# More landing buffers for stored sums, a merge by token halves and halved low parts in an encoder layer's kernel

## The chip, the cores and the metric

The kernel runs on one core of a Trainium2 chip. The metric is the device time of one launch in microseconds. The engines are named as in the profile: PE multiplies matrices, DVE, ACT and POOL work on vectors, SP issues every DMA of this kernel. Each engine takes its instructions in a fixed order.

## The reference

One encoder layer is computed for a prompt of 512 tokens and for a sample of 1024 tokens with the same weights, all in float32. Two attention branches, each 512 wide, are gated, projected to 1024 channels, merged and projected once more. Cut to what matters here:

```python
h = rmsnorm(x, norm_g)
qa, ka, va, za, qb, kb, vb, zb, ga, gb = jnp.split(h @ w_in, np.cumsum(SPLITS)[:-1], axis=-1)
...
oa = neighbourhood_attention(qa, ka, va, rpb_a) * jax.nn.silu(za)
oa = oa @ w_o_a
...
ob = window_gqa_attention(qb, kb, vb, t5_table, sink_b) * jax.nn.silu(zb)
ob = ob @ w_o_b
merged = jax.nn.sigmoid(ga) * oa + jax.nn.sigmoid(gb) * ob
return x + merged @ w_out
```

Queries and keys are normalised per head before the scores. The neighbourhood attention adds a learned bias per offset of rows and columns, the windowed attention a bias per distance and a sink.

## The kernel before

**Products.** A float32 matrix product is made of three matmuls in the faster format fp32r. Each operand is split into a high part (ACT copies it, L602, L1170) and a low part (DVE or POOL subtracts the high part from the original, L607, L1175). The three matmuls are high by high, high by low, low by high; in the dense stages these are L1288, L1289 and L1290 of `product`, and one such step covers 128 of the contracted channels and 512 tokens. Weights land in `raw` (4 buffers) or, for attention, in `w` (128x768) and are split into `whi` and `wlo` (6 buffers each).

**Stages.** In order of time: attention of the prompt (to about 216 us), its dense stages (to 399), attention of the sample (399 to 787), and the sample's dense stages: the z gates (787 to 830), the merge gates g (830 to 966), the merge (966 to 1054) and the output projection (1054 to 1132). Work of two stages overlaps where data allow; some products of g and z for the sample (the "fill") are made in gaps of its attention.

**Pairs.** z, g and the output are made in pairs of output blocks by `pair_strassen`: seven products p1 to p7 replace eight, and for that both weights and tokens are needed as block sums too. The weight sums are s1 to s4 (L1164, tile S). The token sums of the sample are four blocks T of four 128-channel parts each. They were written to DRAM as t_d early on, and `stored_sums` (L1231) loads each part from t_d into a landing buffer `U` of four (L1240) and splits it into the high and low tiles of T. The T tiles have eight buffers, which u and the sums of the merged result (m_d) use later. For the first z pair p1 is already there (`kept`), so the pair begins with p2, which reads h itself, then three products that read T, and so on; p7 reads h itself again.

**u and merge.** The gated attention result u goes to DRAM (u_d) in `store` (L1512) and comes back in 16 loads, 8 chunks by two halves of the tokens (n), through `ot` (first half) and `fr` (second half), chunk by chunk with both halves in turn (L1672 to L1679). The merge loop (L1700) takes an output block m at a time in the order 0, 4, 1, 5 and so on; for each it splits two weight tiles, makes the products of both halves for both branches, loads g back (L1721), multiplies, adds and splits. After every second block `merged_sums` makes the sums m_d of the pair.

**Order.** The class `Flow` takes the whole program as operations with a priority, a choice of engines with an estimated duration for each, and the values they make, read or hold. `run` plays them through on a model of the engines and so fixes engine and order of every instruction ahead of time. Tiles of tags such as U, T, raw, whi, wlo and w are handed out in turn, as their buffers come free. A change in one duration or priority can therefore move instructions anywhere behind it, also in code that the change does not touch.

Of the kernel before, what the change touches and what calls it, by code (L numbers as in the profile page):

```python
# [10 lines left out]
F32 = mybir.dt.float32  # L11
# [29 lines left out]
P = 128  # L41
# [313 lines left out]
def encoder_kernel(  # L355
# [238 lines left out]
    def att_weights(src, n, prio, engs=("pool", "dve"), place=None, after=()):  # L594

        st, at, new = place or (f.value(wpool, [P, 768], F32, "w32", W32), 0, True)
        hi = f.value(wpool, [P, 768], F32R, "whi", 6)
        lo = f.value(wpool, [P, 768], F32R, "wlo", 6)
        sv = lambda: st.t[:, at : at + n]
        ld = f.dma(lambda: nc.sync.dma_start(sv(), src), 512 * n, prio, after=after, **({"new": [st]} if new else {"hold": [st]}))  # L600
        a = f.op(
            (("act", ACT_(n) + 40),), lambda e: act.activation(hi.t[:, :n], sv(), AF.Copy),  # L602
            prio, new=[hi], hold=[st], after=[ld],
        )

        def emit(e):
            engines[e].tensor_tensor(lo.t[:, :n], sv(), hi.t[:, :n].bitcast(F32), op=ALU.subtract)  # L607

        f.op(
            tuple((e, {"pool": POOL_, "dve": DVE_}[e](n)) for e in engs), emit, prio, new=[lo], use=[hi], hold=[st], after=[a],  # L610
        )
        return hi, lo
# [523 lines left out]
    def dense_phase(geo, hh, hl, h_ops, o_stores, exps_done, start, opened, tp, up, p0, p1, p2, x_t, y_t, classic, fill, after_gates=None, side=None):  # L1136
# [93 lines left out]

        def stored_sums(prio, d, after):  # L1231

            tv, ops = {}, {}
            for j in (1, 2, 0, 3):
                tv[j] = tuple(f.value(tp, [P, 4, nh], F32R, "T", 8) for _ in range(2))
                vh, vl = tv[j]
                for k in range(4):
                    st = tile_("U", 4)
                    dma(
                        lambda st=st, j=j, k=k: nc.sync.dma_start(st.t, d[j, k]), 512 * nh, prio, new=[st],  # L1240
                        after=after(j, k),
                    )
                    ops[j, k] = split(
                        lambda vh=vh, k=k: vh.t[:, k], lambda vl=vl, k=k: vl.t[:, k], lambda st=st: st.t, nh, prio,
                        (vh, k == 0), (vl, k == 0), [st],
                    )
# [77 lines left out]
        def pair_strassen(srcs, post, prio, mov_h, mov_t, seed=None, last=False, kept=None):  # L1324
# [40 lines left out]
            else:  # L1365
# [4 lines left out]
                result(0, 0, p1, mul(1, mov_h(1, 0)))  # L1370
            add(u2, p1, mul(2, mov_t(1)))
# [5 lines left out]
            if not last:  # L1377
                result(0, 1, u4, mul(6, mov_h(1, 1)))
# [18 lines left out]

        def spare(tag):
            return f.value(wpool, [P, nh], F32, tag, {"fc": 1}.get(tag, 2))
# [271 lines left out]
        if not short:  # L1671
            for c in range(8):  # L1672
                for n in halves:
                    st = f.value(wpool, [P, nh], F32, "fr", 2) if n else tile_("ot", n_ot)
                    dma(
                        lambda st=st, c=c, n=n: nc.sync.dma_start(st.t, u_d[c, :, half[n]]), 512 * nh, 10 + c // 4,
                        new=[st], after=stores["u", c, n],
                    )
                    split_u(c, n * nh, nh, st, 10 + c // 4)  # L1679
# [20 lines left out]
        for q in range(8):  # L1700
            m = q if short else q // 2 + 4 * (q % 2)
            prio = 12 + q
            ws = []
            for br in range(2):
                raw = load_raw(w_g[m, 4 + br], prio - 2)
                ws.append(weight_tiles([raw], 4, prio - 0.5)[0])
            for n in halves:
                gs_ = []
                for br in range(2):
# [6 lines left out]
                    m_done[q, n] = product(ps, ws[br], movs, prio, True, True)  # L1716
                    tag, bufs = (("C", n_c), ("ot", n_ot) if short else ("U", 4))[br]
                    g = tile_(tag, bufs) if short or br or m < 4 else spare("fl" if n else "fh")
                    turn = [] if short or br or m < 4 else [m_done[max(q - 2, 0), 0]]
# [18 lines left out]
            if not short and m >= 4:  # L1738
# [203 lines left out]
```

## Time and profile before

| | |
|---|---|
| time before, median of 3 runs | 1135.88 us (1134.05 to 1137.46) |
| time of the profiled execution | 1136.88 us |
| its span | 1135.1 us |
| granted TensorE clock, mean | 1.00 |
| ACT busy, share of span | 653.7 us, 58% |
| POOL busy, share of span | 327.1 us, 29% |
| bytes moved by DMA | 186.11 MB, mean 164 GB/s |

The span is the time from the first to the last instruction in the profile; the launch has 1.8 us around it. A row of a timeline gives start, duration, engine, line, operation and, in brackets, how long the engine had been idle and what it then waited for. Matmuls are pipelined: their durations overlap, and what counts is the distance of their starts. In rows of waits the numbers are the total, how often, and the longest. In the rows of one line's operations the three durations are the least, the median and the greatest in ns.

### The profile page before, as it was taken

What the parts mean: (1) busy time and instruction counts of PE and PEld (TensorE: products, weight loads), DVE (VectorE), ACT (ScalarE), POOL (GpSimd) and SP (SyncE); (2) the same over time, 40 slices, a digit from 0 to 9 for tenths busy, and PEclk for the clock granted to TensorE, in tenths of its full rate; (3) what the DMA queues carried; (4) which work ended last, traced back from release to release, by engine and by line L of the source; (5) the groups of instructions that cost most, each with busy time, mean ns of one, the idle gap of its engine ahead of it and who ended that gap; (6) DMA issues with size and microseconds to landing.
All of it is one profiled execution on the core that took longest, in us unless ns stands there. A gap on an engine that the chain in (4) does not pass through costs nothing.

```text
span 1135.1 us, 18686 instructions
## 1 busy us (share of the span) xinstructions
PE 1121.6 (99%) x6079; PEld 973.9 (86%) x6079; DVE 863.8 (76%) x1995; ACT 653.7 (58%) x1498; POOL 327.1 (29%) x432
## 2 busy tenths in 40 slices
PE   8999999999999999999999999999999999999998
PEld 6999988888888889999899988988788888788887
DVE  5888797587765468887868888885888866779874
ACT  6777987644433246574759888876534434522440
POOL 4654433000010044433414344420033221124221
PEclk9999999999999999999999999999999999999999
DMA  7854533488786422121312314244958645868982
GB/s 261 273 157 139 183 115 103 110 262 260 241 276 196 159 91 72 29 79 29 91 32 84 82 38 112 57 131 127 300 187 244 218 167 180 297 219 281 302 279 93
DMA packets 139108, 186.11 MB, mean 164 GB/s; under 512 B 29897, under 2 KB 68561, under 8 KB 139010
## 3 DMA queue, kind: packets, MB, share of 16 engines
q1 hardware_dynamic: 139010, 184.91, 51.4%
q8 instruction: 48, 0.79, 0.3%
q14 instruction: 50, 0.41, 0.1%
HBM read 138.71 MB, written 50.88 MB: 167 GB/s over the span
## 4 chain that ended last, share of the span: by engine, by line
PE 89%; DMA 4%; DVE 4%; ACT 1%; issue 1%; SPq 0%; POOL 0%; DVEq 0%; POOLq 0%; ACTq 0%
PE p L761 25%; PE x L1288 8%; PE x L1290 8%; PE x L1289 8%; PE x L1063 5%; PE x L1026 5%; PE x L934 5%; PE d L1288 4%; PE d L1289 4%; PE d L1290 4%; PE p L1289 4%; PE p L1290 4%; PE p L1288 4%; PE x L861 2%; DMA ot<-u_d 1%
## 5 line engine op out<-in xcount | busy, mean ns | idle before, releaser
L761 PE MATMUL p<-whi,hh 128*128 128x384 f32 x384 | 133.6, 348 | 0.0
L761 PE MATMUL p<-whi,hl 128*128 128x384 f32 x384 | 132.4, 345 | 0.0
L761 PE MATMUL p<-wlo,hh 128*128 128x384 f32 x384 | 132.2, 344 | 0.0
L978 ACT ACTIVATE sb<-sb,mx 128x384 f32<-128x384 f32 (+1 forms) x192 | 107.7, 565 | 22.9 <-DVE mx L969 22.6
L1170 ACT ACTIVATE whi<-raw 128x512 fp32r<-128x512 f32 (+1 forms) x136 | 79.4, 599 | 67.4 <-PE x L1289 46.3
L1289 PE MATMUL x<-T,whi 128*128 128x512 f32 x284 | 110.7, 390 | 0.3 <-DVE T L1175 0.2
L1288 PE MATMUL x<-T,whi 128*128 128x512 f32 x284 | 110.6, 390 | 0.0
L1290 PE MATMUL x<-T,wlo 128*128 128x512 f32 x284 | 110.5, 389 | 0.0
L761 PE MATMUL p<-whi,hb 128*128 128x384 f32 x384 | 107.8, 346 | 0.0
L1037 DVE TENSOR_TENSOR pp<-x,pp 128x512 fp32r<-128x512 f32 (+1 forms) x136 | 82.6, 639 | 20.3 <-ACT pp L1032 19.2
L1175 DVE TENSOR_TENSOR wlo<-raw,whi 128x512 fp32r<-128x512 f32 (+1 forms) x109 | 73.3, 682 | 26.5 <-ACT whi L1170 26.0
L1175 POOL TENSOR_TENSOR wlo<-raw,whi 128x512 fp32r<-128x512 f32 (+1 forms) x27 | 32.1, 1199 | 172.9 <-ACT whi L1170 160.2
L799 POOL TENSOR_TENSOR rs_r<-rs_v,mhalf 128x4 f32<-128x4 f32 (+1 forms) x72 | 79.9, 1109 | 5.7
L1032 ACT ACTIVATE pp<-x 128x512 fp32r<-128x512 f32 (+1 forms) x136 | 70.9, 561 | 18.2 <-PE x L1026 17.1
L792 POOL TENSOR_SCALAR rs_v<-ss 128x4 f32<-128x4 f32 (+1 forms) x72 | 26.0, 361 | 185.1 <-DVE ss L785 181.7
L1063 PE MATMUL x<-pp,v 128*128 128x256 f32 (+1 forms) x368 | 76.6, 322 | 0.0
L1288 PE MATMUL x<-hh,whi 128*128 128x512 f32 x196 | 76.4, 390 | 0.1
L1290 PE MATMUL x<-hh,wlo 128*128 128x512 f32 x196 | 76.3, 389 | 0.0
L1289 PE MATMUL x<-hl,whi 128*128 128x512 f32 x196 | 76.2, 389 | 0.0
L761 PEld LDWEIGHTS p<-whi,hl 128*128 128x128 f32 x384 | 72.8, 190 | 1.3 <-issue 1.0
L761 PEld LDWEIGHTS p<-whi,hh 128*128 128x128 f32 x384 | 73.0, 190 | 1.1 <-issue 0.5
L761 PEld LDWEIGHTS p<-wlo,hh 128*128 128x128 f32 x384 | 72.9, 190 | 0.9 <-issue 0.5
(381 smaller groups left out, 3011.9 us busy)
## 6 DMA issues: line engine op xcount, KB each, us to landing
raw<-in_w_g_dram SPq DMA_DIRECT2D x84, 256.0 KB
w<-in_w_att_dram SPq DMA_DIRECT2D x46, 384.0 KB
raw<-in_w_z_dram SPq DMA_DIRECT2D x40, 256.0 KB
ot<-o_d SPq DMA_DIRECT2D x36, 256.0 KB
raw<-in_w_out_dram SPq DMA_DIRECT2D x36, 256.0 KB
g_d<-C SPq DMA_DIRECT2D x34, 256.0 KB
fr<-in_w_g_dram SPq DMA_DIRECT2D x28, 256.0 KB
out_dram<-C SPq DMA_DIRECT2D x19, 256.0 KB
```

Of the source, the lines that this page charges most:

```text
L761: pe.matmul(ps.t[:, :GW], part[u](k), mv.t[:, c], start=k == 0 and m == 0, stop=k == KC - 1 and m == 2,)
L799: lambda e: nc.gpsimd.tensor_tensor(r.t[:, :nn], rv.t[:, :nn], mhalf[:, :nn], op=ALU.pow),
L934: pe.matmul(pss[2 * pair + i].t[:, :width], q.t[rows, u, at : at + P], kv[:, tiles[0] : tiles[-1] + 1 : step], start=n == 0, stop=n == 2,)
L978: act.activation(sb.t[:, :width], sb.t[:, :width], AF.Exp, bias=mx.t[:, i : i + 1], scale=-1.0, accum_out=sm.t[:, i : i + 1],)
L1032: lambda e, pt=pt, pp=pp, nn=nn: act.activation(pp.t[:, 0, :nn], pt.t[:, :nn], AF.Copy),
L1037: lambda e, pt=pt, pp=pp, nn=nn: dve.tensor_tensor(pp.t[:, 1, :nn], pt.t[:, :nn], pp.t[:, 0, :nn].bitcast(F32), op=ALU.subtract),
L1063: pe.matmul(out(), v.t[:, vs], mv(), start=first, stop=last)
L1170: (("act", ACT_(n)),), lambda e: act.activation(hi(), src(), AF.Copy), prio,
L1175: lambda e: engines[e].tensor_tensor(lo(), src(), hi().bitcast(F32), op=ALU.subtract), prio,
L1288: pe.matmul(out, hi.t[:, cs], mh(), start=first and k == 0, stop=False, **more)
L1289: pe.matmul(out, hi.t[:, cs], ml(), start=False, stop=False, **more)
L1290: pe.matmul(out, lo.t[:, cs], mh(), start=False, stop=last and k == len(ws) - 1, **more)
```

## The change

The change has five parts. In the code `short` is true for the prompt and false for the sample, and `here` is true for the pairs of z whose first product was kept in a tile, `prio` being 0 for the first of them.

1. `att_weights`: the low part of an attention weight tile is made by two subtractions of half the width, each of which may go to POOL or DVE by itself.
2. `stored_sums`: for t_d, the parts k = 1 and k = 3 land in the buffers `fh` (2) and `w32` (2, the attention weights' own) in place of U, so eight landing buffers serve in place of four. The loads now also wait for the operation `opened`, which opens the stage's tiles.
3. `pair_strassen`: in the first z pair the seventh product, which reads h and the weight sum s4, is made right behind p2, ahead of the products that read T.
4. The loads of u come back by halves: the first half of all eight chunks, then the second; they land in `fr`, `fh`, `fl` and `ot` by turns, and their priorities follow.
5. The merge goes by turns (m, n): blocks k and k+4 of the first half, then both of the second half. The weights of both blocks are kept for that. The wait that holds back g's loads for m >= 4 is now for the third product from the last.

```diff
@@ -603,12 +603,15 @@
             prio, new=[hi], hold=[st], after=[ld],
         )
 
-        def emit(e):
-            engines[e].tensor_tensor(lo.t[:, :n], sv(), hi.t[:, :n].bitcast(F32), op=ALU.subtract)
-
-        f.op(
-            tuple((e, {"pool": POOL_, "dve": DVE_}[e](n)) for e in engs), emit, prio, new=[lo], use=[hi], hold=[st], after=[a],
-        )
+        for i in range(2):
+            c = slice(i * n // 2, (i + 1) * n // 2)
+            f.op(
+                tuple((e, {"pool": POOL_, "dve": DVE_}[e](n // 2)) for e in engs),
+                lambda e, c=c: engines[e].tensor_tensor(
+                    lo.t[:, c], st.t[:, at : at + n][:, c], hi.t[:, c].bitcast(F32), op=ALU.subtract
+                ),
+                prio, use=[hi], hold=[st], after=[a], **({"into": [lo]} if i else {"new": [lo]}),
+            )
         return hi, lo
 
     def expand_ops(geo, prios, after):
@@ -1228,6 +1231,9 @@
 
             return moving_sums(tv, ops)
 
+        def spare(tag):
+            return f.value(wpool, [P, nh], F32, tag, {"fc": 1}.get(tag, 2))
+
         def stored_sums(prio, d, after):
 
             tv, ops = {}, {}
@@ -1235,13 +1241,13 @@
                 tv[j] = tuple(f.value(tp, [P, 4, nh], F32R, "T", 8) for _ in range(2))
                 vh, vl = tv[j]
                 for k in range(4):
-                    st = tile_("U", 4)
+                    st = spare(("fh", "w32")[k // 2]) if not short and d is t_d and k % 2 else tile_("U", 4)
                     dma(
-                        lambda st=st, j=j, k=k: nc.sync.dma_start(st.t, d[j, k]), 512 * nh, prio, new=[st],
-                        after=after(j, k),
+                        lambda st=st, j=j, k=k: nc.sync.dma_start(st.t[:, :nh], d[j, k]), 512 * nh, prio, new=[st],
+                        after=[*after(j, k), *([opened] if d is t_d else [])],
                     )
                     ops[j, k] = split(
-                        lambda vh=vh, k=k: vh.t[:, k], lambda vl=vl, k=k: vl.t[:, k], lambda st=st: st.t, nh, prio,
+                        lambda vh=vh, k=k: vh.t[:, k], lambda vl=vl, k=k: vl.t[:, k], lambda st=st: st.t[:, :nh], nh, prio,
                         (vh, k == 0), (vl, k == 0), [st],
                     )
             return moving_sums(tv, ops)
@@ -1368,6 +1374,7 @@
                     (("act", ACT_(sn)),), lambda e: act.activation(p1.t, a.t[:, :sn], AF.Copy), prio, new=[p1], use=[a]
                 )
                 result(0, 0, p1, mul(1, mov_h(1, 0)))
+            ps7 = mul(6, mov_h(1, 1)) if here and not prio else None
             add(u2, p1, mul(2, mov_t(1)))
             add(u3, u2, mul(3, mov_t(2)))
             b = mul(4, mov_t(0))
@@ -1375,7 +1382,7 @@
             result(1, 1, u3, b)
             result(1, 0, u3, mul(5, mov_t(3)), ALU.subtract)
             if not last:
-                result(0, 1, u4, mul(6, mov_h(1, 1)))
+                result(0, 1, u4, ps7 or mul(6, mov_h(1, 1)))
                 return
 
             c = seed(0, sn, sn, u4, prio)
@@ -1394,9 +1401,6 @@
                 last_op = f.ops[-1]
                 post(0, nh + s.start, nh // 2, c, False, prio, s.start, [last_op])
 
-
-        def spare(tag):
-            return f.value(wpool, [P, nh], F32, tag, {"fc": 1}.get(tag, 2))
 
         def pairs_apart(jobs, prio, mov_h, mov_t, late, seed=None, ready=()):
 
@@ -1669,14 +1673,15 @@
         if after_gates:
             after_gates()
         if not short:
-            for c in range(8):
-                for n in halves:
-                    st = f.value(wpool, [P, nh], F32, "fr", 2) if n else tile_("ot", n_ot)
+            for n in halves:
+                for c in range(8):
+                    st = spare(("fr", "fh", "fl")[c % 4]) if c % 4 < 3 else tile_("ot", n_ot)
+                    pr = 10 + n + c // 4 / 2
                     dma(
-                        lambda st=st, c=c, n=n: nc.sync.dma_start(st.t, u_d[c, :, half[n]]), 512 * nh, 10 + c // 4,
+                        lambda st=st, c=c, n=n: nc.sync.dma_start(st.t, u_d[c, :, half[n]]), 512 * nh, pr,
                         new=[st], after=stores["u", c, n],
                     )
-                    split_u(c, n * nh, nh, st, 10 + c // 4)
+                    split_u(c, n * nh, nh, st, pr)
 
 
         m_ops, m_vals, m_stores, m_done = {}, {}, {}, {}
@@ -1697,15 +1702,18 @@
                     lambda vd=vd, j=j: nc.sync.dma_start(m_d[j, k], vd.t), 512 * sn, prio, after=[o], hold=[vd],
                 )
 
-        for q in range(8):
-            m = q if short else q // 2 + 4 * (q % 2)
-            prio = 12 + q
-            ws = []
-            for br in range(2):
-                raw = load_raw(w_g[m, 4 + br], prio - 2)
-                ws.append(weight_tiles([raw], 4, prio - 0.5)[0])
-            for n in halves:
+        turns, m_ws, m_prods = [(m, 0) for m in range(8)], {}, []
+        if not short:
+            turns = [(k + 4 * i, n) for k in range(4) for n in range(2) for i in range(2)]
+        for q, (m, n) in enumerate(turns):
+            if True:
+                prio = 12 + q * 8 / len(turns)
                 gs_ = []
+                if m not in m_ws:
+                    m_ws[m] = [
+                        weight_tiles([load_raw(w_g[m, 4 + br], prio - 2)], 4, prio - 0.5)[0] for br in range(2)
+                    ]
+                ws = m_ws[m]
                 for br in range(2):
                     ps = bank(next(tags))
                     vh, vl = uv[br, n]
@@ -1713,10 +1721,10 @@
                         (lambda k=k, vh=vh: vh.t[:, k], lambda k=k, vl=vl: vl.t[:, k], u_ops[br, n, k], [vh, vl])
                         for k in range(4)
                     ]
-                    m_done[q, n] = product(ps, ws[br], movs, prio, True, True)
+                    m_prods.append(product(ps, ws[br], movs, prio, True, True))
                     tag, bufs = (("C", n_c), ("ot", n_ot) if short else ("U", 4))[br]
                     g = tile_(tag, bufs) if short or br or m < 4 else spare("fl" if n else "fh")
-                    turn = [] if short or br or m < 4 else [m_done[max(q - 2, 0), 0]]
+                    turn = [] if short or br or m < 4 else m_prods[-3:-2]
                     dma(
                         lambda g=g, br=br, m=m, n=n: nc.sync.dma_start(g.t, g_d[br, m, :, half[n]]), 512 * nh,
                         prio - 0.5, new=[g], after=[*stores["g", br, m, n], *turn],
@@ -1735,7 +1743,7 @@
                     prio, (hh, None), (hl, None), [a], after=h_reads,
                 )
                 m_vals[m, n] = a
-            if not short and m >= 4:
+            if not short and m >= 4 and n:
                 merged_sums(m - 4, prio)
             if side:
                 side(12 + q)
```

The matmuls stay the same in number. `Flow` gives the following new orders.

The first place is SP at the end of the sample's attention, where the loads of t_d begin; o_d is the attention result, raw the next weights, u_d the gated result. Before:

```order
L1527 DMA ot<-o_d_80 128x512 x2
L1240 DMA U<-t_d 128x512 x3
L1252 DMA raw<-in_w_z_dram 128x512 x2
L1240 DMA U<-t_d 128x512
L1512 DMA u_d_93<-C 128x512
L1527 DMA ot<-o_d_80 128x8x64 x2
L1512 DMA u_d_93<-C 128x512
L1252 DMA raw<-in_w_z_dram 128x512
L1240 DMA U<-t_d 128x512
L1252 DMA raw<-in_w_z_dram 128x512
L1240 DMA U<-t_d 128x512 x3
L1527 DMA ot<-o_d_80 128x8x64 x2
```

With the change (the two w names are landing buffers of the attention weights):

```order
L1531 DMA ot<-o_d_80 128x512 x2
L1246 DMA U<-t_d 128x512
L1246 DMA fh<-t_d 128x512
L1246 DMA U<-t_d 128x512
L1246 DMA w_10532<-t_d 128x512
L1258 DMA raw<-in_w_z_dram 128x512 x2
L1516 DMA g_d_94<-fc 128x512
L1516 DMA u_d_93<-C 128x512
L1531 DMA ot<-o_d_80 128x8x64
L1258 DMA raw<-in_w_z_dram 128x512
L1246 DMA U<-t_d 128x512
L1246 DMA fh<-t_d 128x512
```

The loads of t_d stood in groups of three, one, one and three, with stores of u between them; now the first four stand together, and the second four (to `w_10589`) and the third four follow one another. On PE, 13 steps of the fill and a first product stand between the last product of attention and the first product of this stage that reads h, where there were 2, and 24 steps that read h stand ahead of the first one that reads T, where there were 16.

The second place is SP towards the end of the g gates, where loads of u begin. Before:

```order
L1676 DMA ot<-u_d_93 128x512 x2
L1252 DMA raw<-in_w_g_dram 128x512
L1676 DMA fr<-u_d_93 128x512 x2
L1676 DMA ot<-u_d_93 128x512
L1721 DMA U<-g_d_94 128x512 x2
L1676 DMA ot<-u_d_93 128x512
L1512 DMA g_d_94<-C 128x512
L1252 DMA raw<-in_w_g_dram 128x512
L1721 DMA U<-g_d_94 128x512
L1676 DMA fr<-u_d_93 128x512
L1512 DMA g_d_94<-C 128x512
L1676 DMA fr<-u_d_93 128x512
```

With the change:

```order
L1516 DMA g_d_94<-C 128x512
L1258 DMA raw<-in_w_g_dram 128x512
L1681 DMA fr<-u_d_93 128x512
L1681 DMA fh<-u_d_93 128x512
L1681 DMA fl<-u_d_93 128x512
L1681 DMA ot<-u_d_93 128x512
L1258 DMA raw<-in_w_g_dram 128x512
L1681 DMA fr<-u_d_93 128x512
L1681 DMA fl<-u_d_93 128x512
L1729 DMA U<-g_d_94 128x512
L1681 DMA ot<-u_d_93 128x512
L1729 DMA U<-g_d_94 128x512 x2
```

Ahead of the first row here stood four loads of u, the first two chunks with both halves, and the other twelve follow chunk by chunk, from the first row on. With the change all eight loads of the first half stand ahead of this place, in the two buffers each of `fr`, `fh`, `fl` and `ot`, and the rows here are those of the second half.

The third place is POOL in the middle of the sample's attention: low parts of two attention weights (the w names), the reciprocal roots rs of the head norms, and the scaling of attention weights sb. Before:

```order
L799 TENSOR_TENSOR rs_r<-rs_v,mhalf 128x4
L607 TENSOR_TENSOR wlo<-w_6990,whi 128x768
L607 TENSOR_TENSOR wlo<-w_7007,whi 128x768
L1175 TENSOR_TENSOR fl<-fr,fh 128x512
L1008 TENSOR_TENSOR sb<-sb,rs 128x384 x3
L792 TENSOR_SCALAR rs_v<-ss 128x4
L799 TENSOR_TENSOR rs_r<-rs_v,mhalf 128x4
```

With the change:

```order
L610 TENSOR_TENSOR wlo<-w_6377,whi 128x384
L1079 TENSOR_TENSOR ot__7039<-ot__7039 64x2x128
L610 TENSOR_TENSOR wlo<-w_6391,whi 128x384
L795 TENSOR_SCALAR rs_v<-ss 128x4
L802 TENSOR_TENSOR rs_r<-rs_v,mhalf 128x4
L610 TENSOR_TENSOR wlo<-w_7058,whi 128x384 x2
L610 TENSOR_TENSOR wlo<-w_7112,whi 128x384
```

Two subtractions of 768 columns in a row have become three of 384, the fourth being DVE's, with norm roots ahead of them, and single halves stand further ahead. In all, POOL had 12 such subtractions of 768 columns and has 39 of 384; DVE had 36 and has 57. The scalings sb on POOL go from 27 to 41.

## The prediction

> **What bounds the kernel now.** The page comes first: is any engine free to give?
>
> ```profile
> span 1135.1 us, 18686 instructions
> PE 1121.6 (99%) x6079; PEld 973.9 (86%) x6079; DVE 863.8 (76%) x1995; ACT 653.7 (58%) x1498; POOL 327.1 (29%) x432
> ```
>
> PE is busy in 99% of the span, and the change takes no matmul away. So it can win only what PE loses in gaps, and the page's 1135.1 - 1121.6 = 13.5 us is their sum with the start and the tail. The list of what PE waited for says which gaps these are:
>
> ```profile
> PE x L1799 <- DMA rb<-in_norm_row_dram: 4.6, 1, 4.6
> PE x L861 <- DVE qk L816: 2.6, 3, 1.1
> PE d L1289 <- DVE T L1175: 0.8, 2, 0.4
> ```
>
> The 4.6 us at the start have nothing to do with the change. The rest is small, and this list counts a gap only behind the modelled end of a matmul. Matmuls overlap, so I read losses from starts in the timeline of PE instead. The first z pair of the sample:
>
> ```profile
> 811.13 0.50 PE L1288 MATMUL x<-T,whi 128*128 128x512 f32 x1
> 811.85 0.50 PE L1289 MATMUL x<-T,whi 128*128 128x512 f32 x1 [0.22 <-DVE T L1175]
> ...
> 814.50 0.39 PE L1288 MATMUL x<-T,whi 128*128 128x512 f32 x1
> 815.00 0.50 PE L1289 MATMUL x<-T,whi 128*128 128x512 f32 x1
> 815.34 0.39 PE L1290 MATMUL x<-T,wlo 128*128 128x512 f32 x1
> ...
> 818.77 0.39 PE L1290 MATMUL x<-T,wlo 128*128 128x512 f32 x1
> 818.99 0.39 PE L1288 MATMUL d<-T,whi 128*128 128x512 f32 x1
> 819.73 0.50 PE L1289 MATMUL d<-T,whi 128*128 128x512 f32 x1 [0.35 <-DVE T L1175]
> ...
> 822.35 0.39 PE L1288 MATMUL d<-T,whi 128*128 128x512 f32 x1
> 823.17 0.50 PE L1289 MATMUL d<-T,whi 128*128 128x512 f32 x1 [0.43 <-DVE T L1175]
> ```
>
> Starts stand 0.23 apart when nothing is late (818.77 to 818.99). Four steps are late, by 0.49, 0.27, 0.51 and 0.59, and one start after each comes 0.11 late as well (815.00 to 815.34): 1.86 + 0.44 = **2.3 us**. All four are the second matmul of a step, which reads the low part of a block sum T. Its chain is a DMA from t_d into a U buffer, the high part on ACT, the low part on DVE. The timelines of SP and ACT show why it is late:
>
> ```profile
> 794.26 3.45 SPq L1512 DMA_DIRECT2D u_d<-C  x1
> ...
> 799.25 1.33 SPq L1240 DMA_DIRECT2D U<-t_d  x3
> ...
> 802.27 2.43 SPq L1512 DMA_DIRECT2D u_d<-C  x1
> ...
> 805.76 3.11 SPq L1240 DMA_DIRECT2D U<-t_d  x4
> ```
>
> ```profile
> 810.44 1.25 ACT L1170 ACTIVATE T<-U 128x512 fp32r<-128x512 f32 x2 [3.48 <-DMA U<-t_d]
> ...
> 818.12 2.55 ACT L1170 ACTIVATE T<-U 128x512 fp32r<-128x512 f32 x4 [3.59 <-DMA U<-t_d]
> ```
>
> SP issues in its fixed order. Four U buffers let only four loads be ahead; SP stands 3.11 us at the third four, since they wait for the split of the four before, and 3.45 and 2.43 us at stores of u between them. ACT then sits idle for the loads. The last of the four has a second cause:
>
> ```profile
> 820.31 2.81 DVE L1175 TENSOR_TENSOR T<-U,T 128x512 fp32r<-128x512 f32 x2
> ```
>
> ```profile
> 821.28 1.30 POOL L1175 TENSOR_TENSOR wlo<-S,whi 128x512 fp32r<-128x512 f32 x1 [0.44 <-DMA raw<-in_w_z_dram]
> ```
>
> Two DVE subtractions of 0.69 took 2.81 while one POOL subtraction ran. The same shows in attention, where it makes PE's largest gap there:
>
> ```profile
> 544.21 0.42 DVE L1080 TENSOR_TENSOR ot__6987<-ot__6987 64x256 f32<-64x256 f32 x1
> ...
> 547.39 1.86 DVE L1080 TENSOR_TENSOR ot__7030<-ot__7030 64x256 f32<-64x256 f32 x1
> ```
>
> ```profile
> 547.12 3.81 POOL L607 TENSOR_TENSOR wlo<-w,whi 128x768 fp32r<-128x768 f32 x2 [0.26 <-ACT whi L602]
> ```
>
> ```profile
> 548.21 0.33 PE L761 MATMUL p<-wlo,hh 128*128 128x384 f32 x1
> 548.39 0.34 PE L761 MATMUL p<-whi,hl 128*128 128x384 f32 x1
> 549.73 0.41 PE L861 MATMUL x<-ident,qk 128*128 128x128 f32 x2 [1.00 <-DVE qk L816]
> ```
>
> A DVE multiply of 0.42 takes 1.86, until about the end of the first of POOL's two 768-wide subtractions; the qk multiply stands behind it on DVE, and PE, in 0.18 steps before, loses 1.34 - 0.18 = **1.2 us**. Third, the merge stage:
>
> ```profile
> 966.89 0.63 ACT L1170 ACTIVATE T<-ot 128x512 fp32r<-128x512 f32 x1 [1.45 <-DMA ot<-u_d]
> ```
>
> ```profile
> 969.73 0.39 PE L1290 MATMUL p<-T,wlo 128*128 128x512 f32 x1
> 970.37 0.49 PE L1288 MATMUL p<-T,whi 128*128 128x512 f32 x1 [0.25 <-ACT T L1170]
> 971.10 0.50 PE L1289 MATMUL p<-T,whi 128*128 128x512 f32 x1 [0.23 <-DVE T L1175]
> ```
>
> Steps of 0.64 and 0.73 in place of 0.23, and 0.1 behind: **1.0 us**, since the second token half is wanted 2.7 us (12 matmuls of 0.23) after the first. Last, the output projection:
>
> ```profile
> 1071.77 1.28 ACT L1170 ACTIVATE T<-U 128x512 fp32r<-128x512 f32 x2 [5.09 <-DMA U<-m_d]
> ```
>
> ```profile
> 1076.53 0.39 PE L1290 MATMUL x<-hh,wlo 128*128 128x512 f32 x1
> 1077.02 0.50 PE L1288 MATMUL x<-hh,whi 128*128 128x512 f32 x1
> ```
>
> ACT waits for merged sums while weights it should split stand behind: 0.49 - 0.23 + 0.1 = 0.4 us.
>
> **The change part by part.** *Landing buffers for t_d and the product ahead.* The 16 loads stay 16, on the same queue. Eight can now be under way before a split frees a buffer, and SP meets the first two fours with nothing but old readers of fh and w to wait for. In the new order PE has 13 steps of the gate fill and a first product between the last PV product and the first hh product of this stage (2 before), and 24 steps of hh products (16 before) before the first step that reads T: 19 steps of 3 x 0.23, so 13 us more between the end of attention and the first need of T. PE's work is only moved. The largest lateness summed is 2.3, and the loads' longest hold was 3.6 at ACT; both are well below 13. I take the whole **-2.3**; the bounds are -2.3 and 0. The product moved ahead needs weights s4, the last sum of the pair, whose low part stands on DVE behind five splits of T (5 x 0.69 = 3.5 us); PE's 20 other steps, 13.6 us, cover it. Without that cover it costs those 3.5.
>
> *u in halves, merge by token halves.* Sixteen loads again, but all eight of the first half are issued ahead into four kinds of buffer, and PE's merge goes through (k, n=0), (k+4, n=0) with both branches, then n=1: the second half is wanted after 4 products (48 x 0.23 = 11 us), not 1 (2.7). Later by 8 us where it lacked about 0.7: **-1.0** (bounds -1.0 and 0). Weights of two blocks are held at once, 4 of the 6 buffers of each kind; the next pair's splits then wait for PE, with one block of products (2.7 us) over. The merged sums come once per pair of halves, as before. In the output stage ACT's order now has the weight splits ahead of the wait for m_d: **-0.3** (0 to -0.4).
>
> *Attention's low parts in halves.* One subtraction of 128x768 becomes two of 128x384, on either engine:
>
> ```profile
> L607 POOL TENSOR_TENSOR wlo<-w,whi x12: 1805/1860/2274, 6.5 to 658.1; 128x768 fp32r<-128x768 f32 x12
> ...
> L1175 POOL TENSOR_TENSOR wlo<-raw,whi x27: 739/1287/1762, 157.9 to 1108.2; 128x512 fp32r<-128x512 f32 x20, 128x256 fp32r<-128x256 f32 x7
> L1175 DVE TENSOR_TENSOR wlo<-raw,whi x109: 407/684/1496, 179.8 to 1110.6; 128x512 fp32r<-128x512 f32 x100, 128x256 fp32r<-128x256 f32 x9
> ```
>
> Between 256 and 512 columns POOL goes from 0.74 to 1.29, so 384 cost about 1.02; DVE from 0.41 to 0.68, so 0.55. POOL had 12 wide ones (22.9 us) and has 39 halves (39.8 us); DVE 36 wide ones and 57 halves. POOL also takes 14 more sb multiplies. The stall at 548 came from one hold of a whole POOL instruction; its place now has other instructions around it, so it goes as such, **-1.2** (bounds -1.2 and 0). But new meetings come. Twelve wide ones made one stall of 1.17, where DVE was held 1.44 and so 0.27 were covered. A half holds DVE for 1.44 x 1.02 / 1.86 = 0.79, leaving 0.52; at one in twelve, 39 halves make 3.25 such, 1.7 us. With shorter holds they also meet a waited-for DVE row less often, 1.7 x 0.55 = 0.9. I take **+1.2**, between these; the bounds are 0 and 3.25 x 1.02 = 3.3.
>
> [...]
>
> *Start of sample attention.* In the new order POOL has two pairs rs_v, rs_r ahead of the bias that waits for a mask, but DVE has a bias instruction there, which PE's next qk stands behind.
>
> ```profile
> 405.96 0.71 POOL L695 TENSOR_TENSOR bias<-mask,raw 128x192 f32<-128x192 f32 x1 [1.86 <-DMA mask<-in_mask_s_dram]
> ```
>
> L861's waits are 2.6 us with the 1.0 at 549.73, so 1.6 are others; a wait for one mask changes engine. **-0.2**, bounds -1.5 (all but 0.1 go) and +0.7 (one bias row more in the chain).
>
> *Start and tail* stay: 0.
>
> The sum: -2.3 - 1.0 - 0.3 - 1.2 - 0.2 + 1.2 = **-3.8 us**. The profiled execution took 1136.88 (span 1135.1 and 1.8 around it), which makes 1133.1; it lies 1.00 above the median 1135.88, so against the median it is **1132.1**.
>
> **The rivals.** *Attention gives it back.* POOL's added time holds DVE at the upper bound, +3.3: 1135.88 - 4.8 - 0.2 + 3.3 = 1134.2. For it: DVE is held whole instructions; the order of all of attention is changed, not only L607's. Against: DVE is 76% busy, and only one of twelve reached PE. *The change doesn't do what it says in the dense part.* The loads are late because the transfers themselves are slow, not for want of a buffer, and the gaps at T and u stay: 1132.1 + 3.3 = 1135.4; with half of them, 1133.8. For it: all loads go through one SP queue. Against: SP's 3.11 at the third four is a wait for buffers. *Slower: SP stands at the first fh load.* It waits for PE's last read of fh in the gate fill, and the store of g right behind waits for ACT; raw z weights are queued behind both. If it is held as long as its longest stall here, 3.45, and the eight loads by 0.44 (799.25: 1.33 for 3) stand ahead of weights, these come 3.45 + 3.5 = 7 us later; PE's 13 steps cover 13 x 0.69 = 9. So nothing shows until the cover falls below 7, as it would if the fill ran earlier; with none, the z term's 2.3 stay as well, and the time is 1132.1 + 2.3 + 7 = 1141.4.
>
> **How the numbers follow.** Forecast 0.56, attention gives it back 0.18, transfers too slow 0.16, SP stands 0.10. The measurement tells about 0.3%, 3.4 us, from no change, so the line is at 1132.5, just above my time: of the forecast's case 0.46 lie below it; 0.02 of the others do. Within 0.3% are 0.10 + 0.31 = 0.41; slower 0.11, the last rival and 0.01 of the second. The low end has all gains at their bounds and no new stall: 2.3 + 1.0 + 0.4 + 1.2 + 1.5 = 6.4, 1129.5, rounded to 1129. The high end takes in both middle rivals at once, with half of the dense gaps (+1.7) and the added bias row at its bound (+0.9): 1134.2 + 2.6 = 1136.8.
>
> **What would show it.** Right: the PE rows that read T in the first z pair 0.23 apart; SP's U and fh loads from t_d without a stall of 3 us; no wait at p<-T when the merge begins; DVE rows held under 1 us in attention. Wrong: waits of x L864 on qk over 2.6 us in total, or PE waiting for whi at the head of the first z pair, or a gap at the product with s4.

## The result and the profile after

| | before | with the change |
|---|---|---|
| median | 1135.67 us (6 runs) | 1144.76 us (6 runs, 1139.41 to 1145.91) |
| ratio | 1 | 1.007, 95% interval 1.0048 to 1.0093 |
| profiled execution, span | 1136.88, 1135.1 | 1144.78, 1143.0 |

The change made the kernel slower by 0.7%, 9 us; 1132.1 had been predicted, with a range of 1129 to 1136.8. Ratios here and below leave out two executions that lie far off, one of `halves_c3ot3` (1290.4 us at a granted clock of 0.852) and one of the kernel before (3512.53 us). The page of the changed kernel begins:

```profile
span 1143.0 us, 18771 instructions
PE 1124.1 (98%) x6079; PEld 975.6 (85%) x6079; DVE 859.4 (75%) x1991; ACT 652.9 (57%) x1494; POOL 370.5 (32%) x488
```

PE has the same 6079 matmuls and 7.9 us more span, so the loss is again in gaps and, behind two of them, in slow matmuls. The list of what PE waited for begins (total, times, longest):

```profile
PE x L1807 <- DMA rb<-in_norm_row_dram: 4.3, 1, 4.3
PE p L1295 <- DVE hl L1178: 2.7, 1, 2.7
PE x L864 <- DVE qk L819: 1.9, 3, 0.7
PE x L1294 <- ACT hh L1173: 1.5, 1, 1.5
PE x L1294 <- ACT fh L1416: 1.5, 1, 1.5
PE x L532 <- DVE xt L520: 0.8, 1, 0.8
PE d L1294 <- DVE fc L1612: 0.8, 1, 0.8
PE x L1029 <- DVE mx L972: 0.5, 1, 0.5
```

The waits for low parts of T (DVE T L1175 before) are gone, as predicted. New ones are `hl` and `hh`, the merged values that the output projections read, and `fh`, a copy out of a bank of the output projection. Where in time the 7.9 us came is seen by the start of the same matmul, counted from the first, in both traces:

| matmul no. | stage it falls in | before | after | later by |
|---|---|---|---|---|
| 1691 | first step on T, prompt | 307.39 | 309.70 | 2.3 |
| 2000 | output projection, prompt | 377.44 | 383.67 | 6.2 |
| 4585 | ahead of the first step on T, sample | 791.34 | 796.11 | 4.8 |
| 4750 | behind the z pairs, sample | 831.24 | 834.28 | 3.0 |
| 5500 | merge, sample | 1002.28 | 1004.28 | 2.0 |
| 6000 | output projection, sample | 1116.37 | 1124.30 | 7.9 |

Up to matmul 4585 both kernels have made the same products, so attention and z can be told apart there. The sample's attention won 1.5, z won 1.7 and u 1.0, in sum near the prediction. The prompt lost 6.2, of which 2.3 before its dense stages' first step on T, and the last stage 5.9. The PE timeline of the changed kernel shows the gap in the prompt's output projection, and what follows it:

```profile
357.75 0.39 PE L1296 MATMUL x<-hh,wlo 128*128 128x512 f32 x1
359.68 0.50 PE L1294 MATMUL x<-hh,whi 128*128 128x512 f32 x1 [1.54 <-ACT hh L1173]
360.40 0.50 PE L1295 MATMUL x<-hl,whi 128*128 128x512 f32 x1 [0.23 <-DVE hl L1178]
...
361.71 0.63 PE L1294 MATMUL x<-hh,whi 128*128 128x512 f32 x1
362.13 0.63 PE L1295 MATMUL x<-hl,whi 128*128 128x512 f32 x1
```

A gap of 1.93 - 0.23 = 1.7 and one of 0.5; then matmuls start 0.43 apart in place of 0.23, eight of them, 1.6 us more. The merged values hh are late. SP issues the first load of g for the prompt's merge 6.5 us later, before and then after:

```profile
310.31 0.45 SPq L1721 DMA_DIRECT2D ot<-g_d  x1
```

```profile
316.78 0.65 SPq L1729 DMA_DIRECT2D ot<-g_d  x1
```

In the sample's output projection:

```profile
1061.63 0.50 PE L1294 MATMUL p<-hh,whi 128*128 128x512 f32 x1
1064.83 0.80 PE L1295 MATMUL p<-hl,whi 128*128 128x512 f32 x1 [2.69 <-DVE hl L1178]
...
1091.23 0.39 PE L1296 MATMUL d<-hh,wlo 128*128 128x512 f32 x1
1093.10 0.50 PE L1294 MATMUL x<-hh,whi 128*128 128x512 f32 x1 [1.49 <-ACT fh L1416]
```

3.2 - 0.23 = 3.0 us, slow matmuls behind, and later 1.65. The timelines of SP show what changed ahead of that. Loads of the output projection's weights, before and then after:

```profile
1042.65 2.34 SPq L1252 DMA_DIRECT2D raw<-in_w_out_dram  x3
1046.39 0.37 SPq L1252 DMA_DIRECT2D raw<-in_w_out_dram  x1
1054.12 3.68 SPq L1252 DMA_DIRECT2D raw<-in_w_out_dram  x4
```

```profile
1050.83 3.01 SPq L1258 DMA_DIRECT2D raw<-in_w_out_dram  x4
1071.01 3.46 SPq L1258 DMA_DIRECT2D raw<-in_w_out_dram  x4
```

The last two fours come 8 and 17 us later, 6 and 15 with PE's own delay of 2 taken off. The first of them arrives while DVE, ACT and POOL finish the last merged block (DVE, ACT, POOL of after):

```profile
1058.82 1.67 DVE L1167 TENSOR_TENSOR fl<-fl,U 128x512 f32<-128x512 f32 x1
1061.35 1.76 DVE L1167 TENSOR_TENSOR S<-raw,S 128x512 f32<-128x512 f32 x1
1063.03 1.75 DVE L1178 TENSOR_TENSOR hl<-fl,hh 128x512 fp32r<-128x512 f32 x1
```

```profile
1060.97 0.61 ACT L1173 ACTIVATE hh<-fl 128x512 fp32r<-128x512 f32 x1
```

```profile
1058.64 1.29 POOL L1167 TENSOR_TENSOR S<-raw 128x512 f32<-128x512 f32 x1 [2.81 <-DMA raw<-in_w_out_dram]
1061.14 1.42 POOL L1178 TENSOR_TENSOR T<-U,T 128x512 fp32r<-128x512 f32 x1 [1.20 <-ACT T L1173]
1062.52 1.71 POOL L1167 TENSOR_TENSOR S<-raw 128x512 f32<-128x512 f32 x1
```

S are the weight sums. On DVE one of them stands between the merged sum and its low part hl, and all three DVE rows take 1.7 where 0.68 is usual, each beside a POOL row and ending 0.55 after that row's end: 3 x 1.0 us.

### The profile page after: what moved, and what is told of

It is laid out like the page before. It is cut to its first block, busy times and chain, and to the rows that moved or that the text cites. A ratio compares the mean times of both kernels' runs of the same rounds, so it can differ in the third digit from the quotient of the medians.

```text
span 1143.0 us, 18771 instructions
## 1 busy us (share of the span) xinstructions
PE 1124.1 (98%) x6079; PEld 975.6 (85%) x6079; DVE 859.4 (75%) x1991; ACT 652.9 (57%) x1494; POOL 370.5 (32%) x488
## 4 chain that ended last, share of the span: by engine, by line
PE 80%; DMA 6%; DVE 4%; ACT 2%; issue 1%; SPq 1%; POOL 1%; DVEq 0%; ACTq 0%; POOLq 0%
PE p L764 20%; PE x L1294 8%; PE x L1295 8%; PE x L1296 8%; PE x L1066 5%; PE x L1029 5%; PE x L937 4%; PE p L1295 4%; PE p L1296 4%; PE p L1294 4%; PE d L1294 4%; PE d L1296 3%; PE d L1295 3%; PE x L864 1%; DMA raw<-in_w_out_dram 1%
## 5 line engine op out<-in xcount | busy, mean ns | idle before, releaser
L1294 PE MATMUL x<-T,whi 128*128 128x512 f32 x280 | 108.9, 389 | 0.0
L1295 PE MATMUL x<-T,whi 128*128 128x512 f32 x280 | 108.9, 389 | 0.0
L1178 POOL TENSOR_TENSOR wlo<-raw,whi 128x512 fp32r<-128x512 f32 (+1 forms) x29 | 38.3, 1326 | 211.7 <-ACT whi L1173 211.7
L1294 PE MATMUL x<-hh,whi 128*128 128x512 f32 x200 | 78.9, 394 | 3.5 <-ACT hh L1173 1.5
L1295 PE MATMUL x<-hl,whi 128*128 128x512 f32 x200 | 78.6, 393 | 0.2 <-DVE hl L1178 0.2
L764 PEld LDWEIGHTS p<-whi,hb 128*128 128x128 f32 x384 | 69.1, 188 | 3.7 <-issue 1.3
```

Of the source, the lines that this page charges most:

```text
L764: pe.matmul(ps.t[:, :GW], part[u](k), mv.t[:, c], start=k == 0 and m == 0, stop=k == KC - 1 and m == 2,)
L1178: lambda e: engines[e].tensor_tensor(lo(), src(), hi().bitcast(F32), op=ALU.subtract), prio,
L1294: pe.matmul(out, hi.t[:, cs], mh(), start=first and k == 0, stop=False, **more)
L1295: pe.matmul(out, hi.t[:, cs], ml(), start=False, stop=False, **more)
```

## The experiments

Each was timed in turns with the kernel before on one chip; the ratios are to that. Gaps are read from starts of PE's matmuls in the profiled execution. "Part" counts as in the change's list.

**Part 1 alone, and the rest without it.** `halves_only` is the kernel before with the first hunk of the change's diff, `no_halves` the changed kernel without that hunk:

```diff
-        f.op(
-            tuple((e, {"pool": POOL_, "dve": DVE_}[e](n)) for e in engs), emit, prio, new=[lo], use=[hi], hold=[st], after=[a],
-        )
+        for i in range(2):
+            c = slice(i * n // 2, (i + 1) * n // 2)
...
```

> The kernel before with part 1 alone (low parts of attention weights in halves). Its order on every engine is that of the changed kernel up to the end of the sample's attention. Theory A (the halves cost time in the prompt and win it back only in part in the sample's attention): the prompt's dense stages end 6 us later than before, with a PE gap of about 1.7 us and slow matmuls behind it near 358 us; the sample's attention takes 2 to 3 us less than before; the time is 1138 to 1140. Theory B (part 1 is harmless, the loss lies in parts 2 to 5): within 1.5 us of before, 1134 to 1137.

Measured: 1140.28, ratio 1.0043 (1.0025 to 1.0061), just above Theory A's range. The gap at the prompt's output projection is there (2.5 and 0.5 us, slow matmuls behind), none over 1.0 in the sample's.

> Parts 2 to 5 without part 1. The order is that of the kernel before up to the end of the sample's attention. Theory A, with a loss of its own in the output projection from the merge by token halves: the z gaps (2.3) and the u gaps (1.0) go, the gap at the first product on the last merged blocks comes (3 to 6 us): 1135 to 1139. Theory B: all of the loss, 1142 to 1146. Rival C (the output loss comes with the halves, since these change what stands where at the end of attention): 1131 to 1133.

Measured: 1141.65, 1.005 (1.0034 to 1.0066). No gap in the prompt; 2.9 and 2.5 us in the sample's output projection. The time is above Theory A's range and just below Theory B's, so it doesn't decide by itself; the places of the gaps do. There are two separate losses: one comes with part 1 and lies in the prompt, one comes with parts 2 to 5 and lies at the end. Theory B falls, since part 1 alone loses too, and so does rival C.

**Parts 2 and 3, parts 4 and 5.** `z_only` has the hunks of `stored_sums` and `pair_strassen`, `merge_only` those of u and the merge.

> Parts 2 and 3 alone (landing buffers for t_d, product p7 ahead in the first z pair). If the prediction's z term is right: the four late T steps of the first z pair are gone, 2.3 us, less a new gap of 0.6 at the moved product: 1133.5 to 1134.5; no gap over 1 us in the output projection.

> Parts 4 and 5 alone (u by halves, merge by token halves). If the merge order makes the loss in the output projection: the two u gaps (1.0) go, and a PE gap of 2 to 3 us at hl of the last merged block comes, with matmuls at half rate behind it: 1138 to 1141. If the loss comes from parts 2 and 3 or from the halves: 1134 to 1135.

Measured: `z_only` 1136.51, 1.0004 (0.9994 to 1.0015), nothing gained, against the expectation. `merge_only` 1141.8, 1.0048 (1.0032 to 1.0063), with both gaps at the end, here 2.9 each:

```profile
PE x L1288 <- ACT fh L1412: 2.7, 1, 2.7
PE p L1289 <- DVE hl L1175: 2.7, 1, 2.7
```

Parts 4 and 5 make the late loss. In z a gap of 1.2 had come in the place of most of the four; counted as in the prediction, 1.7 us are lost in the pair in place of 2.3, and 1.6 at the first products on u in place of 1.0 (PE, DVE, POOL of `z_only`):

```profile
810.28 0.39 PE L1291 MATMUL d<-T,whi 128*128 128x512 f32 x1
811.69 0.50 PE L1292 MATMUL d<-T,whi 128*128 128x512 f32 x1 [1.02 <-DVE T L1175]
```

```profile
809.05 0.90 DVE L1164 TENSOR_TENSOR ot<-ot 128x512 f32<-128x512 f32 x1 [0.80 <-DMA ot<-o_d]
809.87 1.76 DVE L1175 TENSOR_TENSOR T<-w,T 128x512 fp32r<-128x512 f32 x1
```

```profile
809.35 1.73 POOL L1175 TENSOR_TENSOR wlo<-raw,whi 128x512 fp32r<-128x512 f32 x1
```

The load of T is in time now, and the low part is late instead: on DVE it stands behind a row that waited 0.80 for a load of o_d, and it takes 1.76 beside a POOL row, where 0.68 is usual.

**What in the merge makes the late loss.** Theory R: by token halves the merge holds four of the six tiles of whi and wlo; they are handed out in turn, a pair of the output projection takes two, so its weights, raw loads and sums come one pair later. Theory P: POOL holds DVE (the three DVE rows under the result: 1.7 in place of 0.68), whatever for. `merge_first` and `merge_sdve` start from `merge_only`; `psum=True` leaves DVE as the only choice for the weight sums of the output projection:

```diff
-            turns = [(k + 4 * i, n) for k in range(4) for n in range(2) for i in range(2)]
+            turns = [(k + 4 * i, n) for k in range(1) for n in range(2) for i in range(2)] + [(k + 4 * i, n) for k in range(1, 4) for i in range(2) for n in range(2)]
```

> Parts 4 and 5 alone, but the merge goes by token halves only for the first pair of blocks (0, 4); the other pairs go block by block as before, so at the end of the merge two weight tiles of each kind are held in place of four. Theory R (the tiles held for two blocks make the output projection's weights one pair late, and their sums meet the last merged block): the two gaps in the output projection (4.5 and 4 us with slow matmuls) are gone, u waits at most 0.7: 1134 to 1136. Theory P (they come from POOL instructions that hold DVE, whichever weights these are for): a gap of 2 us or more at hl of the last merged block stays, 1139 to 1142.

```diff
-                        pr - 0.5 + (j == 1), new=[out], use=[in0, in1],
+                        pr - 0.5 + (j == 1), psum=True, new=[out], use=[in0, in1],
```

> Parts 4 and 5 alone, and the weight sums s1 to s4 of the output projection made on DVE only; POOL keeps other work there. Theory P: the first gap (2.9 us at hl of the last merged block) falls below 1 us and no slow matmuls follow; the time falls by 3 to 5 us to 1137 to 1139. Theory R: the weights are as late as before, so the second gap (2.9 us, PE waiting behind ACT's copy into fh) stays and the first at most halves: 1139 to 1142.

Measured: `merge_first` 1135.98, 1.0005 (0.9996 to 1.0014); the gaps are 0.4 and 1.0, the u gaps are gone. `merge_sdve` 1138.81, 1.0031 (1.0019 to 1.0043): the time lies in Theory P's range, the gaps fit neither theory as I had put it. A gap of 2.9 stays at the first product on the last block, now not at hl: PE waits for ACT's copy out of a bank, which stands behind the split of a weight sum that DVE has made late. The second gap is gone. The rows are PE, ACT and SP of `merge_sdve`, then SP of `merge_only`:

```profile
1060.68 0.50 PE L1288 MATMUL p<-hh,whi 128*128 128x512 f32 x1 [2.71 <-ACT fr L1412]
```

```profile
1059.52 0.63 ACT L1170 ACTIVATE whi<-S 128x512 fp32r<-128x512 f32 x1 [1.67 <-DVE S L1164]
1060.05 0.58 ACT L1412 ACTIVATE fr<-p 128x512 f32<-128x512 f32 x1
```

```profile
1048.76 2.37 SPq L1252 DMA_DIRECT2D raw<-in_w_out_dram  x4
1058.79 4.40 SPq L1252 DMA_DIRECT2D raw<-in_w_out_dram  x4
```

```profile
1048.29 3.20 SPq L1252 DMA_DIRECT2D raw<-in_w_out_dram  x4
1068.80 3.15 SPq L1252 DMA_DIRECT2D raw<-in_w_out_dram  x4
```

So the edit did not leave the weights where they were. One four of loads is as late as in `merge_only`, and the first gap stays; the last four is issued 10 us sooner, and the second gap is gone. That fits R, but it was seen only afterwards. Since the order of the merge itself changed in `merge_first`, a third run keeps it and holds fewer tiles:

```diff
...
+                        four = weight_tiles(
+                            [load_raw(w_g[m + 4 * i, 4 + br], prio - 2) for i in range(2) for br in range(2)], 6, prio - 0.5
+                        )
+                        m_ws[m], m_ws[m + 4] = four[:2], four[2:]
...
```

> Parts 4 and 5 alone with the merge by token halves throughout, but the weights of the two blocks that are held together are packed six to a tile, so three tiles of each kind are held in place of four. In its order four more loads of the output projection's weights stand ahead of the last stores of merged sums. Theory R (tiles held make these weights late): the gaps in the output projection fall from 8 to 9 us with slow matmuls to under 3: 1135 to 1138. If it is the order of the merge itself (last block later, sums together), the gaps stay: 1140 to 1143.

Measured: 1133.98, 0.9988 (0.9976 to 1.0), better than R's range. No wait over 0.2 us is left behind 830 us, neither at u nor in the output projection. The last two fours of weight loads are issued from 1037.01 to 1046.34 and at 1058.20, and PE's order is that of `merge_only` up to matmul 5911. Three tiles held in place of four take away the whole loss, with the same merge order and POOL at work: R holds. That POOL's holds are how part of it reaches PE is read from the three DVE rows of 1.7 us in the changed kernel and was not tested apart.

**What in part 1 makes the early loss.** `halves_c3ot3` gives the prompt's merge a third `ot` buffer at the cost of one `C`; `halves_s` gives `att_weights` a number of parts, one in the prompt's attention and two in the sample's:

```diff
-        n_c, n_ot = (4, 2) if short else (5, 2)
+        n_c, n_ot = (3, 3) if short else (5, 2)
```

> Part 1 alone, and in the prompt's dense stages three buffers C and three ot in place of four and two. Theory A1 (the prompt's merge runs as a loop through the two ot buffers: load of g, sigmoid, multiply, add, next load, and in the new order it starts too late for the output projection): with a third ot the loop runs ahead, the gap near 357 us (2.5 and 0.5 us, slow matmuls behind) is gone: 1134 to 1136. Theory A2 (the start of the merge, not its pace, is late): the gap stays over 1 us: 1138 to 1141.

```diff
...
+                    1 if nt == NT_P else 2,
...
```

> Part 1 in the sample's attention alone; the prompt's attention keeps full width. Theory: the loss of part 1 lies in the prompt, 2.5 us of new waits of PE on DVE in its attention and the gap at its output projection; without it the sample's attention gains about 1 us: 1133.5 to 1136. If the loss is in the sample as well: over 1137.

Measured: `halves_c3ot3` 1138.04, 1.0019 (1.0005 to 1.0033): no gap is left near 357 us, as Theory A1 has it, but it stays above its 1134 to 1136. The edit changed the start of the merge too: its first load of g is issued at 313.64, and at 317.05 in `halves_only`, so pace and start are not parted by this run alone. The rest lies in the prompt's attention. PE's waits between 14 and 216 us, in the kernel before and in the changed one:

```profile
PE x L861 <- DVE qk L816: 0.5, 1, 0.5
```

```profile
PE d L1294 <- DVE fc L1612: 0.8, 1, 0.8
PE x L864 <- DVE qk L819: 0.7, 1, 0.7
PE x L1029 <- DVE sb L1013: 0.4, 1, 0.4
PE p L764 <- DVE hb L667: 0.2, 1, 0.2
```

All four kernels with halves in the prompt reach matmul 1691 at 308.4 to 311.0 us, the other fourteen at 305.8 to 307.8: 2.8 us on average. `halves_s` is 1133.89, 0.9986 (0.9974 to 0.9999): without the prompt part 1 gains.

**The parts together.** `all_first` is the whole change with the turns of `merge_first`, `no_halves_first` the same without part 1, `halves_s_first` with part 1 in the sample only.

> The whole change, but the merge by token halves only for the first pair of blocks. If the two losses are separate, this takes away the one in the output projection and keeps the one in the prompt: 1137 to 1140, with the gap near 357 us and no gap over 1 us after 1040 us. If the output projection's gaps come from the halves in attention as well: 1141 to 1145.

> Parts 2 to 5 without the halves, the merge by token halves for the first pair of blocks only. The z gaps fall by 0.5 to 2 and the u gaps by 0.5 to 1 us, and neither loss is there: 1133.5 to 1135.5.

> All five parts, the halves in the sample's attention alone and the merge by token halves for the first pair of blocks only: what the prediction wanted of the change without the two losses. z -1.7, u -1.0, sample's attention -1: 1131.5 to 1134; no PE gap over 1.3 us after the start. If parts that gain alone lose again together: 1135 to 1138.

Measured: 1138.46, 1.0026 (1.0012 to 1.0039), with the prompt's gap and one of 1.2 near 1077; 1136.16, 1.0007 (0.9995 to 1.002), a z gap of 1.4 and one of 2.0 near 1075; 1132.2, 0.9979 (0.9968 to 0.9989). `all_first` and `halves_s_first` lie in the expected ranges of time, though with gaps that weren't expected (1.2 near 1077; 1.9 in the prompt of the profiled execution, which is the slowest of twelve, 1136.84). `no_halves_first` lies above its 1133.5 to 1135.5: the gap of 2.0 stays in the output projection, with slow matmuls behind it, and, as in `z_only`, parts 2 and 3 gain little in z without the halves (1.55 us lost in the pair, 2.3 before).

**Which z part, and the repaired change.** `land_only` has part 2, `p7_only` part 3. `halves_s_pack` is the whole change with the edits of `halves_s` and `merge_pack`; `halves_s_pack_c3` has the ot edit too.

> Part 2 alone, the landing buffers for t_d. If the gaps in the first z pair came from too few buffers: at most 0.8 us lost there, 1134 to 1135. If a DVE that is held by POOL takes the place of the loads: 1.5 us or more stay and the time is within 0.7 us of before.

> Part 3 alone, the product p7 ahead in the first z pair. It gives the loads 2.7 us more: if they are late by no more than 0.6 each, as the rows of before say, the gaps at T go, 1134 to 1135; if each later load slips with the buffers that are freed later, about 1.5 to 2.3 us stay, 1135 to 1136.5.

> All five parts, the halves in the sample's attention alone, the merge by token halves throughout with its weights packed six to a tile. If the two causes are all of the loss: halves_s lies 1.8 us and merge_pack 1.7 us below the kernel before, and z adds up to 1.5: 1130 to 1133. If a third cause exists in the parts together: 1134 to 1138.

> The same with three C and three ot buffers in the prompt's dense stages. If the gap at the prompt's output projection comes from the pace of the ot loop, none is there in any run and no run has a granted clock under 1.0 for it: median 1130 to 1132.5, highest run under 1135. Rival: fewer C buffers cost as much elsewhere in the prompt: 1133 to 1136.

Measured: `land_only` 1135.99, 1.0002 (0.9989 to 1.0015), 2.6 us still lost in the pair; `p7_only` 1135.49, 1.0006 (0.9993 to 1.0018), 1.7 lost (2.3 before, counted the same way). `halves_s_pack` **1130.63, 0.9958 (0.9942 to 0.9975)**; `halves_s_pack_c3` 1130.65, 0.9955 (0.9938 to 0.9972), highest run 1131.18. Both are faster than either kernel. What PE still waits for in `halves_s_pack`:

```profile
PE x L1814 <- DMA rb<-in_norm_row_dram: 4.5, 1, 4.5
PE x L864 <- DVE qk L819: 1.3, 2, 0.8
PE x L1029 <- DVE mx L972: 0.5, 1, 0.5
PE x L532 <- DVE xt L520: 0.3, 1, 0.3
```

Nothing in the sample's dense stages is left of it.

## Why the prediction was wrong, step by step

Two steps failed, one at the end and one in the prompt.

- **Output projection, "-0.3": +5.9.** This is the first step that failed: what the held tiles cost the stage behind the merge was put at nothing. The prediction did see that four of six weight tiles are held, but asked only whether "the next pair's splits" in the merge have time, "with one block of products (2.7 us) over". The same tiles are the output projection's, so its weights came one pair later: its last two fours of loads, 6 and 15 us. `merge_only` shows the loss alone, `merge_pack` and `merge_first` take it away.
- **The prompt, "start and tail stay: 0" and one term of +1.2 for all new meetings: +6.2.** This is the second: what part 1 does to the prompt's order was left out. Apart from that one term, all were sought in the sample. Part 1 also orders the prompt's attention and through it the SP queue of its merge. The first load of g for that merge comes 6.5 us later. The last merged value is ready when PE has waited 1.7 us; the two gaps and the slow matmuls behind them make 3.9 of the 6.2. The attention's own part, 2.8 us on average, lies within the bound of 3.3, but by another mechanism: the four rows above are waits of DVE in a new order and not whole instructions held by POOL (the qk row at 28.81 begins after POOL's rs_r and takes its usual 0.42; fc at 142.99 takes 0.69, sb at 70.52 0.35 and hb at 120.79 0.71, each within 0.03 of the median of its line and shape). In this profile they make 2.1 in place of 0.5, so some of the 2.3 is in smaller pieces that were not followed.
- **A gap can cost more than its length.** Two of the three long gaps of the changed kernel have slow matmuls behind them: 2.2 + 1.7, and 3.0 + 1.7 (1.2 in six slow matmuls, 0.5 in the starts beside them). The third, 1.65, has none.
- **z, -2.3: 1.7, and not by its reason alone.** PE still loses 0.7 in that pair, in the steps on h ahead of the first one on T. Parts 2 and 3 alone give nothing; only with the halves, whose order puts 13 steps of the fill between attention and the pair, is the cover of 13 us there. Without part 1 there are still 2 steps there, and two steps on T stand ahead of the last eight on h. In the profiles the pair loses 1.5 to 1.65 us in the three kernels with part 1 and without parts 2 and 3, and 0 to 0.75 in the five with all three. The prediction named this cover and booked its gain to the buffers.
- **u, -1.0: right** (2.0 at matmul 5500 after 3.0 at 4750), and `merge_pack` keeps it. Beside parts 2 and 3 without the halves (`no_halves`) 0.8 is still lost there.
- **Sample's attention, -1.2 - 0.2 + 1.2:** 1.5 won (4.8 at matmul 4585 after 6.2 at 2000), where 0.2 had been expected. The first term was right: the gap of 1.2 near 548 stands in all ten profiles without part 1 and in none of the eight with it. Of new meetings one is in all eight: near 745 PE loses 0.7 behind two multiplies of sb on DVE, which take 2.81 beside POOL's low parts of gate weights, where one usually takes 0.42. Where the rest of the 1.5 was won isn't shown. `halves_s`, with part 1 in the sample alone, gives 1.8 in all.
- **Rivals.** "Attention gives it back", 1134.2, named a loss that is there, but in the prompt and by another mechanism. "Transfers too slow", 1135.4, needs the gaps at T and u to stay, and they went. "SP stands at the first fh load" was the only one with a slower time, 1141.4, and the nearest in number, but it didn't happen: its fh rows take at most 0.53.

```profile
788.67 0.38 SPq L1246 DMA_DIRECT2D fh<-t_d  x1
...
795.09 0.53 SPq L1246 DMA_DIRECT2D fh<-t_d  x1
```

Left open is what makes the first load of g late. Sixteen of the eighteen profiled kernels have two `ot` buffers in the prompt. In the five of them with the gap that load is issued at 312.88 or later, in the eleven without it at 312.08 or earlier. Two of the five, `merge_only` (313.04, gap 1.6) and `halves_s_first` (312.88, gap 1.9), have the prompt's order free of halves; the other three are those with halves. `halves_c3ot3`, with three `ot` buffers, issues it at 313.64 and has no gap. So the gap goes with a late first load where there are two buffers. A run that delays this load and nothing else wasn't made.

## What to carry to other kernels

A buffer that is held longer is paid for by the next stage that takes from the same ring, so follow the ring past the stage that is changed, to the loads behind it in the queue. Where a planner orders the whole program, a local edit is an edit of all of it: compare the new order in stages that the edit doesn't touch, and run each part alone before the sum. Here the halves and the merge by token halves paid only once each was repaired (1.8 and 1.7 us, barely clear of the noise). That the landing buffers and the product moved ahead pay beside the halves is read from the gaps in z; no run has the two repairs without them.

## What was not expected of the hardware

A gap of PE can be followed by matmuls at half rate. Of thirteen gaps of 1.5 to 3.0 us in eight profiles, nine were followed by five to eight starts 0.43 apart in place of 0.23, four were not (2.9 us in `merge_sdve`, 2.2 in `all_first`, 1.65 and 1.6 elsewhere). The slow stretch begins not always at the gap's end but up to 2 us later (361.71, after 359.68) and ends at 365.08, 3.4 us on; the granted clock from 361.7 to 365.0 is 0.50. The mean granted clock of a profiled execution is 0.997 with two such stretches (the changed kernel), 0.998 or 0.999 with one (`halves_s_first`, `halves_only`) and 0.999 or 1.000 with none (`land_only`, `merge_sdve`), and the changed kernel's runs go from 1139.41 at 1.000 to 1145.91 at 0.997. In the changed kernel a gap of 1.7 us, with one of 0.5 behind it, had such a stretch after it, and one of 1.65 had none. No run here shows what decides whether a gap is followed by one.
